# A tuned encoder layer: the transposed normalised input begins 192 bytes further on in its place

## The chip, the cores and the metric

The kernel runs on one core of one Trainium2 chip. A core has five engines that run side by side: TensorE (PE) multiplies matrices out of SBUF into PSUM, VectorE (DVE) and ScalarE (ACT) work element by element, GpSimd (POOL) does small vector work and issues some transfers, and SyncE (SP) issues most transfers. SBUF is the core's working memory: 128 partitions, each a row of bytes; a tile begins at the same byte in all of them. The metric is the device time of one execution in microseconds (us); of several runs the median counts.

## The reference

One layer of an encoder over 512 positions with 1024 channels, in float32. Its parts, shortened:

```python
u = rms_norm(h, g_mix)                       # (512, 1024)
z = u @ w_in                                 # one projection, columns split into:
q_a, k_a, v_a, q_b, k_b, v_b, f_b, gate_logits = split(z)
y_a = sliding_window_attention(q_a, k_a, v_a, sinks) @ w_br_swa
y_b = forgetting_attention(q_b, k_b, v_b, f_b + b_forget) @ w_br_fox
gates = sigmoid(gate_logits)                 # two per channel
h = h + (gates[0] * y_a + gates[1] * y_b) @ w_mix_out
u = rms_norm(h, g_mlp);  h = h + square(relu(u @ w_ff1)) @ w_ff2
h = h + sigmoid(rms_norm(h, g_ple) @ w_ple_gate) * (p @ w_ple_proj)
out = rms_norm(h, g_final)
```

Here it matters that the first `u` feeds every column of `w_in`: queries, keys, values, forget logits and gates.

## The kernel before

**Precision.** Every float32 operand of a large product is split into a rounded part `h` and a remainder `l`, and a product is three matmuls: high with high, high with low, low with high (`mm3`, lines 75 to 78). So `u` is kept transposed as two halves of one tile, `uh` and `ul`, each `[128 channels of a block, 8 blocks, 512 positions]`. This tile is called `u1` here; its name in the profile is `u`, as for the later `u2` and `u3`, which take the same place when it is free. Names such as `u25h` and `u25l` are something else: the split weights of unit 25. A unit is one weight block, and the units are prepared in a fixed order by `advance` and `emit_split` (ScalarE line 329, VectorE line 330).

**Stages in which `u1` is used.** The order of TensorE's instructions is written out by hand (`manual_schedule`).

1. *V stage*, until about 42 us. The input is normalised, transposed on TensorE (line 387) and written into `u1` by `hi_lo` (lines 72 and 73). `v_mm` (line 483) computes the values and forget logits: here blocks of `u1` are the weights that TensorE loads, and the tiles `wv_h` and `wv_l` stream through, 320 columns into `va` and 328 into `vb`, 192 matmuls in all.
2. *Prefetch*, `fill` with `mm3` into `pf`, lines 76 to 78, until 210 us. 21 chunks (keys, queries, and eight gate chunks), each of 8 blocks times 3 matmuls with 512 columns: a weight unit is loaded and a row block of `u1` streams through, 504 matmuls. The first 64 or so run in one piece; most of the others fill the gaps between the steps of sixteen attention heads (transposes line 827, scores line 769, values line 839), 9 to 18 at a time; the last two chunks run after the heads.
3. *Gates*, `win_mm`, line 918, from 232 to 271 us. The remaining gate columns are computed by a scheme with seven products (numbered `pn` 1 to 7) in place of eight, in blocks of 256 positions: 14 units of 24 matmuls with 256 columns. Products 1, 2 and 4 stream parts of `u1` itself (units 25, 26, 27, 30, 37, 38); products 5 and 6 stream the tile `u1_65` (units 28, 29, 31, 32), products 7 and 3 the tiles `u1_7` and `u1_3` (units 33 to 36), which `gate_ops` makes from `u1` on VectorE and ScalarE (lines 971 to 985, 72, 73).

After that the place is taken by `u_mix` (operands of the mix product, and one early weight block), by `u2` (the MLP's input) and at last by `u3`.

**Places.** Tiles get their bytes from pools that are stacked in order. As built, with the remainder of the first byte by 256:

| tile | first byte of the partition | remainder |
|---|---|---|
| `u1` (32 960 bytes, of which 32 768 hold data) | 17 088 | 192 |
| split weights `u0h`, `u0l`, ... (eight places, 4096 bytes apart) | 66 752 and on | 192 |
| `attn6` (attention output, streamed at lines 76 to 78 into `psy`) | 107 712 | 192 |
| `u1_65` | 182 144 | 128 |
| `u1_7`, `u1_3` | 140 992 and on | 192 |
| parts of `u_mix` | 17 088 + 192 and on | 128 |
| `wv_h`, `wv_l` | rows of 2592 bytes | eight different ones |

The place of `u1` is 48 words (`SHIFT`, 192 bytes) longer than its data. All row blocks of `u1` are 2048 bytes long, so each has the remainder of the first.

Of the kernel before, what the change touches and what calls it, by code (L numbers as in the profile page):

```python
# [15 lines left out]
S = 512  # L16
D = 1024
NT = S // P
KT = D // P
# [25 lines left out]
SHIFT = 48  # L45
# [7 lines left out]
def layer_kernel(ctx: ExitStack, tc: tile.TileContext, x, p, g_mix, w_in, b_forget, swa_sinks,  # L53
# [38 lines left out]
    def cols(w, c0, n, name):  # L92

        src = w[:, c0:c0 + n * P].rearrange("(k q) c -> q k c", q=P)
        r = add_raw([(slice(0, KT), src)], [P, KT, n * P], name)
        return [(r, (slice(None), slice(None), slice(j * P, (j + 1) * P)), [P, KT, P])
                for j in range(n)]
# [27 lines left out]
    for c2 in range(2):  # L125
        q = cols(w_in, C_QB + c2 * 256, 2, f"wqb{c2}")
        k = cols(w_in, C_KB + c2 * 256, 2, f"wkb{c2}")
# [271 lines left out]
    def new_uT(name):  # L399
        t = up.tile([P, 2 * KT * S + SHIFT], F32R, tag="u", bufs=1, name=name)  # L400
        if name == "u2":
            return t
        t = t[:, :2 * KT * S].rearrange("q (e k s) -> q e k s", e=2, k=KT)
        return t[:, 0], t[:, 1]


    psA = ctx.enter_context(tc.tile_pool(name="psA", bufs=2, space=PSUM))
    uh, ul = new_uT("u1")
    r_st = ctx.enter_context(ExitStack())
    glp = r_st.enter_context(tc.tile_pool(name="glp", bufs=1, side="right"))  # L410
# [82 lines left out]
    with tc.manual_schedule(engines={ET.Activation, ET.DVE, ET.SP}):  # L493
# [23 lines left out]
        for half in range(2):  # L517
            ps = psA.tile([P, S], F32, tag="sc", bufs=3, name=f"g_ps{half}")
            for j in range(4):
                k = half * 4 + j  # L520
# [625 lines left out]
    def new_u2():  # L1146

        u2 = new_uT("u2")
        n2 = 1024 + SHIFT
        for n, pn in enumerate((1, 4)):  # L1150
            first = [u2[:, 512 * n + 256 * e:512 * n + 256 * e + 256].rearrange("q (k s) -> q k s", k=1)
                     for e in range(2)]
            rest = [u2[:, n2 + 768 * e:n2 + 768 * e + 768].rearrange("q (k s) -> q k s", k=3)
                    for e in range(2)]
            u_op[pn] = [list(t) for t in zip(first, rest)]
            n2 += 1536
        for pn in (2, 6):
            u_op[pn] = [[u2[:, n2 + 1024 * e:n2 + 1024 * e + 1024].rearrange("q (k s) -> q k s", k=4)]
                        for e in range(2)]
            n2 += 2048  # L1160
# [217 lines left out]
    def t3(tb):  # L1378
        if tb == 0:
            u3["h"], u3["l"] = new_uT("u3")  # L1380
        to_uT(h_sb[:, tb, :], u3["h"], u3["l"], tb, psA, f"n3_{tb}", "sc")
# [109 lines left out]
    for n, st_ in enumerate(steps):  # L1491
        res = None
        if done is not None:
            if done[0] == "f1":
                res = win_out(done[:2], done[2], tmp)
                if res is not None:
                    src, dst, i, e = res
# [140 lines left out]
```

## Time and profile before

| | |
|---|---|
| median of 3 runs | 711.93 us (711.64 to 712.57) |
| profiled execution | 711.02 us, span from the first to the last instruction 709.3 us |
| mean granted clock of TensorE | 0.996 |
| busy: TensorE, its weight loads | 698.0 us (98%), 620.1 us (87%) |
| busy: VectorE, ScalarE, GpSimd | 551.2 us (78%), 457.2 us (64%), 88.7 us (13%) |
| matmuls | 4205 |

How its rows are read: a row of instructions gives line, engine, operation, `out<-in` by the program's tile names without buffer numbers, shapes, and the count; then busy time, mean duration in ns, and the idle time before them with what ended it. A timeline row begins with the start and the length in us. A matmul's duration holds its way through the array, and the next one begins before it ends; the distance between two starts is what it costs the engine. The chain of waits is the sequence of work that ended last, each piece reached from what released the next.

### The profile page before, as it was taken

The page shows a single profiled execution, that of the slowest core. Times are in us where ns is not written, and L with a number is a line of the kernel's source. Part 1 is how long each engine was busy: PE and PEld are TensorE (multiplying, and loading weights), DVE is VectorE, ACT ScalarE, POOL GpSimd, SP SyncE. Part 2 cuts the span into 40 slices and gives each one's busy share as a digit, 9 for nine tenths or more (in the row PEclk, how much of TensorE's full clock was granted, in tenths as well). Part 3 has the DMA queues.
Part 4 walks back from the last instruction along what each step waited for, and adds up shares of the span by engine and source line. Part 5 has one row for each costly group of instructions (what it writes and reads, how often), then busy time and mean ns, then how long its engine had stood idle before and what let it go on. Part 6 is the DMA issues. An engine that isn't in the chain of part 4 may idle for free.

```text
span 709.3 us, 11507 instructions
## 1 busy us (share of the span) xinstructions
PE 698.0 (98%) x4205; PEld 620.1 (87%) x4205; DVE 551.2 (78%) x942; ACT 457.2 (64%) x851; POOL 88.7 (13%) x128
## 2 busy tenths in 40 slices
PE   8999999999999999999999999999999999999996
PEld 7988888888888998888899889988998899988785
DVE  6557888876597666878999985899579966997565
ACT  6547888779962564447788646874487547875452
POOL 1011211100001200211300102010200020010101
PEclk9999999999999999999999999999999999999998
DMA  9256456670355798497885698739995699268003
GB/s 294 66 162 159 106 140 151 149 193 17 120 177 120 136 289 285 94 245 244 204 221 185 119 294 168 244 78 266 182 254 120 170 230 225 94 144 296 1 7 113
DMA packets 75288, 119.88 MB, mean 169 GB/s; under 512 B 6872, under 2 KB 44768, under 8 KB 75232
## 3 DMA queue, kind: packets, MB, share of 16 engines
q1 hardware_dynamic: 66016, 86.25, 38.7%
q0 software_dynamic: 8928, 32.51, 24.8%
q8 instruction: 33, 0.54, 0.3%
q10 hardware_dynamic: 288, 0.39, 0.2%
q14 instruction: 23, 0.19, 0.1%
HBM read 72.93 MB, written 4.19 MB: 109 GB/s over the span
## 4 chain that ended last, share of the span: by engine, by line
PE 89%; DVE 6%; issue 2%; DMA 2%; ACT 1%; POOL 0%; SPq 0%; POOLq 0%; DVEq 0%; ACTq 0%
PE pf L76 5%; PE pf L78 5%; PE pf L77 5%; PE (0, 's2')x L1304 3%; PE mxx L1304 3%; PE (2, 's2')x L1304 3%; PE (1, 's2')x L1304 3%; PE h_sc L769 3%; PE h_pv L839 2%; PE h_tr L827 2%; PE psy L76 2%; PE psy L78 2%; PE psy L77 2%; PE va L483 2%; PE vb L483 2%
## 5 line engine op out<-in xcount | busy, mean ns | idle before, releaser
L303 POOL DMA_DIRECT2D wq<-wq x35 | 30.4, 941 | 218.1 <-DVE u43l L330 30.5
L787 ACT ACTIVATE s<-s,h_nm 128x128 f32<-128x128 f32 (+1 forms) x64 | 32.6, 511 | 6.0 <-DVE h_nm L780 5.2
L73 DVE TENSOR_TENSOR h_ptl<-h_tr,h_pth 128x512 fp32r<-128x512 f32 (+2 forms) x40 | 22.9, 604 | 3.9 <-ACT h_pth L72 3.4
L72 ACT CAST h_pth<-h_tr 128x512 fp32r<-128x512 f32 (+2 forms) x40 | 19.5, 523 | 1.8 <-PE h_tr L827 1.5
L368 POOL TENSOR_SCALAR n_ms<-acc 128x1 f32<-128x1 f32 x15 | 6.9, 460 | 105.4 <-ACT junk L1136 45.8
L483 PE MATMUL va<-wv_h,u 128*128 128x320 f32 x64 | 20.0, 317 | 0.0
L303 POOL DMA_DIRECT2D wgw<-wgw x8 | 7.1, 968 | 101.6 <-DVE u25l L330 77.7
L827 PE MATMUL h_tr<-ident,s 128*128 128x128 f32 x136 | 19.6, 277 | 0.2
L483 PE MATMUL vb<-wv_h,u 128*128 128x328 f32 x64 | 19.6, 313 | 0.0
L839 PE MATMUL h_pv<-h_ptl,v 128*128 128x256 f32 (+1 forms) x64 | 16.9, 305 | 0.4 <-DVE h_ptl L73 0.3
L839 PE MATMUL h_pv<-h_pth,v 128*128 128x256 f32 (+1 forms) x64 | 17.3, 290 | 0.0
L1540 DVE TENSOR_TENSOR sgp<-sgp,pp 128x512 f32<-128x512 f32 (+1 forms) x9 | 5.7, 632 | 14.5 <-ACT sgp L1539 14.5
L827 PEld LDWEIGHTS h_tr<-ident,s 128*128 128x128 f32 x136 | 15.0, 141 | 2.0 <-DVE h_ao L849 0.5
L1136 ACT ACTIVATE junk<-h_sb 128x512 f32<-128x512 f32 x16 | 10.0, 631 | 9.7 <-DVE h_sb L1128 7.0
L807 ACT ACTIVATE s<-s,h_rec 128x128 f32<-128x128 f32 (+2 forms) x32 | 14.2, 482 | 2.3 <-DVE h_rec L801 2.3
L849 DVE TENSOR_TENSOR h_ao<-h_pv,h_ao 64x512 f32<-64x512 f32 x16 | 10.9, 682 | 6.1 <-ACT h_ao L848 5.8
L801 DVE RECIPROCAL h_rec<-h_den 128x4 f32<-128x4 f32 x16 | 3.0, 185 | 14.5 <-ACT s L787 14.3
L775 DVE CUSTOM_DVE_ANT_0 s<-h_sc,causal 128x128 f32<-128x128 f32 (+3 forms) x32 | 13.8, 484 | 0.3 <-PE h_sc L769 0.3
L1539 ACT ACTIVATE sgp<-psgt,rs 128x512 f32<-128x512 f32 x7 | 4.8, 685 | 14.2 <-PE psgt L78 14.2
L839 PEld LDWEIGHTS h_pv<-h_ptl,v 128*128 128x128 f32 x64 | 12.1, 188 | 1.7 <-DVE h_ptl L73 0.8
L73 DVE TENSOR_TENSOR u<-n_tr,u 128x512 fp32r<-128x512 f32 x16 | 10.5, 685 | 3.9 <-ACT u L72 3.9
L775 DVE CUSTOM_DVE_ANT_0 s<-h_sc,bswa 128x256 f32<-128x256 f32 (+1 forms) x32 | 10.7, 384 | 3.1 <-PE h_sc L769 3.1
(1645 smaller groups left out, 2779.9 us busy)
## 6 DMA issues: line engine op xcount, KB each, us to landing
wq<-in_w_ff_dram SPq DMA_DIRECT2D x43, 512.0 KB, 5.9
wq<-wq POOLq DMA_DIRECT2D x35, 512.0 KB, 5.6
wq_c<-in_w_ff_dram SPq DMA_DIRECT2D x9, 512.0 KB, 6.2
wg<-in_w_in_dram SPq DMA_DIRECT2D x4, 1024.0 KB, 5.6
wgw<-in_w_in_dram SPq DMA_DIRECT2D x8, 512.0 KB, 4.9
wgw<-wgw POOLq DMA_DIRECT2D x8, 512.0 KB, 5.8
wq<-in_w_mix_out_dram SPq DMA_DIRECT2D x8, 512.0 KB, 5.2
wpg<-in_w_ple_gate_dram SPq DMA_DIRECT2D x4, 1024.0 KB, 7.7
```

The lines of the kernel that those rows point to most:

```text
L73: nc.vector.tensor_tensor(lo, src, hi.bitcast(F32), ALU.subtract)
L76: nc.tensor.matmul(ps, lh, rh, start=start, stop=False)
L77: nc.tensor.matmul(ps, lh, rl, start=False, stop=False)
L78: nc.tensor.matmul(ps, ll, rh, start=False, stop=stop)
L303: nc.gpsimd.dma_start(q, other, accum_op=ALU.add)
L483: nc.tensor.matmul(ps, u[:, kk_, ts_], w[:, kk_, c0:c1], start=kk_ == 0 and n == 0, stop=kk_ == KT - 1 and n == 2)
L769: nc.tensor.matmul(ps[:, off:off + n], qs[i][z][:, qb * P:(qb + 1) * P], kk[i][z][:, k0:k0 + n], start=z == 0, stop=z == 1)
L775: nc.vector.tensor_tensor_reduce(out=s[:, o:o + n], in0=ps[:, off:off + n], in1=c["bias"](qb), scale=1.0, scalar=NEG, op0=ALU.add, op1=ALU ...
L787: nc.scalar.activation(sl, sl, AF.Exp, bias=nm[:, qb:qb + 1], accum_out=den[:, qb:qb + 1])
L827: nc.tensor.transpose(tr[:, n, :], c["s"][:, o, :], ident)
L839: nc.tensor.matmul(pv[:, q0:q0 + nq, :], V2[kb][:, c["v"], :], t[:, o:o + nq, :], start=n == 0, stop=n == 2 * NT - 1, skip_group_check=True)
L1304: nc.tensor.matmul(bank[bkey, bk, i], o, w, start=tg != "" and n == 0, stop=n == 5, skip_group_check=True)
```

## The change

`new_uT` makes the tile of the transposed input and cuts it into `uh` and `ul`. For `u1` the cut now begins at word 48 of the place in place of word 0; `u3` begins at word 0 as before.

```diff
     def new_uT(name):
         t = up.tile([P, 2 * KT * S + SHIFT], F32R, tag="u", bufs=1, name=name)
         if name == "u2":
             return t
-        t = t[:, :2 * KT * S].rearrange("q (e k s) -> q e k s", e=2, k=KT)
+        n = SHIFT if name == "u1" else 0
+        t = t[:, n:n + 2 * KT * S].rearrange("q (e k s) -> q e k s", e=2, k=KT)
         return t[:, 0], t[:, 1]
```

`u1` then begins at byte 17 280, with remainder 128. Every other tile stays where it was. The program has the same instructions in the same order with the same waits; in 840 matmuls, 16 VectorE and 8 ScalarE instructions the address of the operand in `u1` is 48 words higher.

## The prediction

> **What bounds the kernel now.** I read the busy times first, then the waits of TensorE, then the chain of waits, and last the timeline of single matmuls.
>
> ```profile
> PE 698.0 (98%) x4205; PEld 620.1 (87%) x4205; DVE 551.2 (78%) x942; ACT 457.2 (64%) x851; POOL 88.7 (13%) x128
> ...
> PE 89%; DVE 6%; issue 2%; DMA 2%; ACT 1%; POOL 0%; SPq 0%; POOLq 0%; DVEq 0%; ACTq 0%
> ```
>
> TensorE (PE) is busy 98% of the span and holds 89% of the chain that ended last. The tile `u1` is in use until 271 us, so the next rows are TensorE's stretches there (us, busy, matmuls, clock, DMA share, GB/s) and its only wait between 40 and 272 us.
>
> ```profile
> 40.00:56.00 16.00, 16.00 (x77) 1.00 0.55 136
> 56.00:199.00 143.00, 142.42 (x795) 1.00 0.48 125
> 199.00:231.00 32.00, 32.00 (x143) 1.00 0.60 165
> 231.00:271.00 40.00, 40.00 (x337) 1.00 0.87 234
> PE h_pv L839 <- DVE h_ptl L73: 0.3, 1, 0.3
> ```
>
> TensorE idles 0.6 us of 231, at the full granted clock. So in this part one matmul follows the other as fast as TensorE takes them, and a nanosecond more or less on each goes to the end time one for one. The question is therefore only what the new address does to the distance from the start of one matmul to the start of the next. The printed durations (389 ns for 512 columns) overlap each other; I use the distance between starts.
>
> **The change part by part.** The two programs have the same instructions in the same order. 864 of them reach `u1` 48 words further on: 840 matmuls, 16 VectorE and 8 ScalarE instructions. No wait, transfer or tile is added or moved. I write an operand's place as its start byte modulo 256, moving operand first, weights second. `u1` goes from 192 to 128; the weight units `u0h`, `u0l` and so on stay at 192.
>
> *First term: the gate matmuls with 256 columns (line 918).* Of 336, 144 stream `u1` itself (units 25, 26, 27, 30, 37, 38), so they go from 192/192 to 128/192. The trace already has both pairs in this stage: units 28, 29, 31 and 32 stream `u1_65`, which lies at 128. Here is the chain of waits, 24 matmuls a row.
>
> ```profile
> 234.76 2.88 PE ('g', 1, 2)x L918 x24
> 237.64 2.88 PE ('g', 0, 2)y L918 x24
> 240.52 2.74 PE ('g', 0, 2)z L918 x24
> 243.26 2.72 PE ('g', 1, 2)z L918 x24
> 245.98 2.86 PE ('g', 1, 2)y L918 x24
> 265.80 2.88 PE ('g', 0, 2)x L918 x24
> ```
>
> Rows 3 and 4 are units 28 and 29: 2.72/24 = 113.3 ns, against 2.88/24 = 120 ns for `u1` (119.2 in unit 30). Units 33 to 36, whose moving tiles lie at 192, take 2.88 too. Over the six `u1` units the starts give 119.8 ns on average, so the gain is 144 x (119.8 - 113.5) = 0.9 us. Could something else become late? TensorE never waits in this stage, and the engines that prepare its weights have room; below are TensorE, its weight loads, VectorE, ScalarE and GpSimd.
>
> ```profile
> 231.00:271.00 40.00, 40.00 (x337) 39.84 (x337) 26.47 (x31) 23.85 (x39) 5.17 (x6) 1.00 0.87 234
> ```
>
> VectorE is busy 26.5 of 40 us and ScalarE 23.9. They must finish each 24-matmul unit 0.15 us sooner, which they do where units 28, 29, 31 and 32 run. If a transfer were late instead (the DMA engines are at 87%), the most that is lost is this 0.9 us.
>
> *Second term: the prefetch matmuls `pf` with 512 columns (lines 76 to 78).* There are 21 chunks of 24, 504 in all, and all of them stream `u1`: 192/192 now, 128/192 then. First what they take now, from the timeline: first start and first start behind the stretch.
>
> ```profile
> 41.78 0.40 PE L76 MATMUL pf<-u,u0h 128*128 128x512 f32 x1
> ...
> 56.09 0.39 PE L76 MATMUL pf<-u,u2h 128*128 128x512 f32 x1
> ...
> 134.08 0.48 PE L76 MATMUL pf<-u,u11h 128*128 128x512 f32 x1
> 134.40 0.40 PE L77 MATMUL pf<-u,u11h 128*128 128x512 f32 x1
> 134.63 0.40 PE L78 MATMUL pf<-u,u11l 128*128 128x512 f32 x1
> 134.87 0.40 PE L76 MATMUL pf<-u,u11h 128*128 128x512 f32 x1
> ...
> 199.09 0.39 PE L76 MATMUL pf<-u,u19h 128*128 128x512 f32 x1
> ...
> 209.97 0.39 PE L76 MATMUL psy<-attn,u21h 128*128 128x512 f32 x1
> ```
>
> In the first stretch 63 matmuls take 14.31 us, 227.2 ns each; in the last 48 take 10.88 us, 226.7 each. In the fills between the attention heads it is less even: behind a transpose the first one takes about 314 (the row at 134.08), and the next ones 224 to 236 until they settle at 227. Added up over all starts: 484 ordinary ones at a mean of 228.8 ns (63 at 227.2, 373 at 229.3, 48 at 226.7), and 20 long ones that follow a transpose and that I leave as they are.
>
> What 128/192 takes at 512 columns is shown in one place only. In the mix stage `u_mix` holds one weight block at 128, streamed against weights at 192, and its rows even agree with the changed `u1` in the byte modulo 2048 (896).
>
> ```profile
> 301.37 2.96 PE L1304 MATMUL mxz<-u_mix,mo 128*128 128x512 f32 x12
> 304.17 0.40 PE L1304 MATMUL mxy<-u47h,u_mix 128*128 128x512 f32 x1
> L1304 PE MATMUL mxz<-u_mix,mo x12: 394/394/397, 301.4 to 303.9; 128*128 128x512 f32 x12
> L1304 PE MATMUL mxx<-u45h,u_mix x8: 388/390/394, 298.6 to 301.1; 128*128 128x512 f32 x8
> L1304 PE MATMUL mxy<-u47h,u_mix x8: 396/397/398, 304.2 to 306.7; 128*128 128x512 f32 x8
> L78 PE MATMUL pf<-u,u1l x8: 389/389/389, 47.7 to 52.5; 128*128 128x512 f32 x8
> ```
>
> The twelve take 304.17 - 301.37 = 2.80 us, 233.3 each, all alike. So the pair that is the quick one at 256 columns is the slow one at 512. I take 233.3: the bytes are the same and so is the number of columns. The cost is 484 x (233.3 - 228.8) = 2.2 us. The bounds come from the nearest rows. Below: no steady stretch of 512 columns is under 226.7, which gives 484 x (226.7 - 228.8) = -1.0 us. Above: 236, the longest that keeps coming back in the fills, gives +3.5 us. Between them lies the mirrored pair 192/128: the row of `u45h` is a mixture of 226, 229 and 232 (229 on average) and the row of `u47h` a steady 233. So two rhythms are possible for one pair, and which one comes depends on what ran ahead. At 229.7 the term would be +0.4 us.
>
> *Third term: the V stage (line 483), where `u1` is the weights.* 192 matmuls load their weights from `u1`; the moving tiles `wv_h` and `wv_l` have rows of 2592 bytes, so the eight row blocks start at eight different places, 32 bytes apart modulo 256.
>
> ```profile
> L483 PE MATMUL va<-wv_h,u x64: 303/311/416, 8.9 to 41.5; 128*128 128x320 f32 x64
> L483 PE MATMUL vb<-wv_h,u x64: 308/312/320, 9.2 to 41.6; 128*128 128x328 f32 x64
> ```
>
> All eight pairs stand in these rows, and the medians of the starts lie within 146 to 150 ns for `va` and 149 to 155 for `vb`. If the distance between the two places counts, moving `u1` by 64 modulo 256 only exchanges the eight distances among the eight blocks; if the moving place counts, it does not change. Both give zero. Bounds: 192 x 5 ns = 1.0 us either way.
>
> *Fourth: the 24 VectorE and ScalarE instructions.* They write `u1` in the V stage and read it for the gate operands.
>
> ```profile
> L73 DVE TENSOR_TENSOR h_ptl<-h_tr,h_pth 128x512 fp32r<-128x512 f32 x24 | 15.8, 683 | 2.1 <-ACT h_pth L72 1.9
> L73 DVE TENSOR_TENSOR u<-n_tr,u 128x512 fp32r<-128x512 f32 x16 | 10.5, 685 | 3.9 <-ACT u L72 3.9
> ```
>
> `h_ptl` lies at 32 and `u` at 192, with the same instruction and the same 683 to 685 ns: I cost it at zero. It also runs beside TensorE work. Were it 5 ns more on each of the 24, that would be 0.1 us even without cover.
>
> The Trainium skill speaks against any effect at all. In "SBUF — State Buffer" (Specifications) it gives 16-byte lines in SBUF, and 192 bytes are twelve whole lines; in "TensorE: Matmul & The Clock Gate" (Part 2: What happens when you issue a matmul, step 1) it says that TensorE reads the weights and the moving operand through two independent ports, so loading the next weights takes nothing from a running matmul. By these the sum would be zero. The trace does not agree: the rows at 240.52 and 245.98 have equal shapes and equal weights' places, and differ by 0.12 us in 24 matmuls.
>
> **The sum.** -0.9 (gates) + 2.2 (`pf`) + 0 + 0 = +1.3 us. The profiled execution took 711.02 us with a span of 709.3; it would become 712.3 with a span of 710.6. It lies 0.9 us under the median of the three runs, 711.93, so the median becomes **713.2 us**. A measurement of this kernel tells about 0.2% (1.4 us) from no change, so the forecast lies just inside "no change", on the slow side.
>
> **The rivals.**
>
> *A. `pf` finds the better rhythm.* Between 229.7 (+0.4 us) and 226.7 (-1.0 us) for `pf`, with the gates' -0.9: -0.5 to -1.9 us, 711.4 to 710.0. For it: the row of `u45h`, where a pair with different places ran at 229, and the fills, which settle at their best rhythm after some ten matmuls. Against it: all twelve of `u_mix` were slow from the first, although they followed `u45`'s mixture.
>
> *B. Slower: the weights' place costs too.* In the V stage every matmul would take one step (6.7 ns) more once its weights lie at 128, as `u47h` with weights at 128 takes 233 against 227: 192 x 6.7 = 1.3 us on top, +2.6 us, 714.5. It decides as soon as it is above 0.1 us, since the rest stands at +1.3. For it: no row of `u_mix` as weights has a median below 390, where plain rows have 389. Against it: the V stage has eight pairs already and none stands out by more than 5 ns.
>
> *C. The place does not matter for 512 columns, nor by itself for 256; what differs is the tile.* Then nothing happens: 711.9. This is the reading to which the two rules of the Trainium skill above lead. For it: only `u_mix` shows the slow pair. Against it: units 33 to 36, other tiles at 192, run at 120 as `u1` does.
>
> *D. `pf` loses a step.* At 256 columns 128/192 takes 6.7 ns less; were it so at 512 (220 ns), `pf` would give 484 x 8.8 = -4.3 us and with the gates -5.2: 706.7. Against it: no stretch of 512 columns anywhere settles under 226.7.
>
> **How the numbers follow.** Forecast 0.52, A 0.26, B 0.11, C 0.07, D 0.04. The forecast's own range, 712.4 to 714.0, lies across the 0.2% bound at 713.35; I give 0.29 of it to no change and 0.23 to slower. A gives 0.14 to no change and 0.12 to faster, B 0.11 to slower, C 0.07 to no change, D 0.04 to faster. Together: faster 0.16, the same 0.50, slower 0.34. The range runs from the good end of A, 710.0, to the forecast's upper edge with B, 714.7; about 0.2 is left outside with D, the edges and the spread of the runs.
>
> **What would show it.** The gate units of `u1` at 2.72 to 2.74 us per 24 in the chain of waits (right) or still 2.88. The `pf` stretch of units 19 and 20: 11.2 us from its first start to that of `psy` (right), 10.9 (A or C) or 10.6 (D). The V stage's rows unchanged in their medians (right) or 5 to 7 ns up (B). The forecast is wrong if `pf` keeps its 389 ns, or if TensorE shows waits between 40 and 272 us that it does not have now.

## The result, and the profile after

The changed kernel takes **714.17 us** (median of 7 runs, 713.34 to 715.51), the kernel before 711.93 beside it (7 runs, 710.51 to 712.77): ratio 1.0034, 95% interval 1.0024 to 1.0044. So it is slower, by 1.7 to 3.1 us by the interval, which is more than the 0.2% that a measurement tells from no change. Predicted were 713.2 us, in a range of 710.0 to 714.7. The profiled execution took 714.12 us with a span of 712.4 (before: 711.02 and 709.3). Of the runs further below, two single ones that took far longer (869.77 us with `u1` at place 0, 2485.57 us with `u1` and the weights moved) are in no ratio.

The busy times from the profile's page, and then TensorE's only wait between 40 and 272 us (who waited, for whom, us in total, times, longest). The insertion of one line shifts the code below it: line 918 is now 919, 839 is 840, 483 is 484; lines 76 to 78 stay.

```profile
PE 701.1 (98%) x4205; PEld 620.8 (87%) x4205; DVE 552.0 (77%) x942; ACT 457.5 (64%) x851; POOL 89.2 (13%) x128
```

```profile
PE h_pv L840 <- DVE h_ptl L73: 0.3, 1, 0.3
```

TensorE is busy 3.1 us longer and the same single 0.3 us wait stands where it stood: nothing has begun to wait in the part that uses `u1`. The time went into the matmuls. First the `pf` stretch of units 19 and 20, from its first start to the first start behind it (timeline: start, printed duration).

```profile
200.67 0.39 PE L76 MATMUL pf<-u,u19h 128*128 128x512 f32 x1
200.90 0.39 PE L77 MATMUL pf<-u,u19h 128*128 128x512 f32 x1
201.14 0.39 PE L78 MATMUL pf<-u,u19l 128*128 128x512 f32 x1
...
211.87 0.39 PE L76 MATMUL psy<-attn,u21h 128*128 128x512 f32 x1
```

48 matmuls take 11.20 us, 233.3 ns each; before they took 10.88, 226.7 each. The gate stage, from the chain of waits (start, us, what; 24 matmuls are one unit; the rows are the units 26, 27, 28, 29 and 37):

```profile
236.64 2.83 PE ('g', 1, 2)x L919 x24
239.47 2.83 PE ('g', 0, 2)y L919 x24
242.29 2.83 PE ('g', 0, 2)z L919 x24
245.12 2.83 PE ('g', 1, 2)z L919 x24
...
267.94 2.74 PE ('g', 0, 2)x L919 x24
```

Units 26 and 27 (rows 1 and 2) went from 2.88 to 2.83 us, and only units 37 (last row) and 38 reach the forecast 2.72 to 2.74. Units 28 and 29 (rows 3 and 4), whose operand `u1_65` was not touched, went the other way, from 2.74 and 2.72 to 2.83. The V stage, where `u1` is the weights, has the same durations within 3 ns in the medians:

```profile
L484 PE MATMUL va<-wv_h,u x64: 303/309/417, 9.0 to 41.8; 128*128 128x320 f32 x64
L484 PE MATMUL vb<-wv_h,u x64: 308/312/320, 9.2 to 41.9; 128*128 128x328 f32 x64
```

The same matmuls matched one to one between the two traces give the delay as it grows: +0.28 us at 34 us, +0.68 at 71, +1.40 at 179, +1.93 at 220 and at 249, +1.83 at 274, +1.82 still at 507; then +2.05 at 529, +2.77 at 618 and +3.09 at 702. At 34 us neither a `pf` nor a gate matmul has run (the V stage has; its 192 starts sum to 30.45 us against 30.34), and behind 271 us no instruction touches `u1`. So between 34 and 274 us the delay grows by 1.83 - 0.28 = 1.55 us, and another 1.3 us arise behind 507 us. The waits of TensorE behind 505 us, first before, then after:

```profile
PE psgt L77 <- DVE u173l L321: 0.3, 1, 0.3
```

```profile
PE psgt L77 <- DVE u173l L321: 0.7, 2, 0.4
PE ('f1', 6)x L919 <- ACT u_('f1', 6)_6525 L930: 0.4, 1, 0.4
```

Some 0.8 us of the late part are these two waits. Whether the change causes them is one of the questions below.

### The profile page after: what moved, and what is told of

It is laid out like the page before. It is cut to its first block, busy times and chain, and to the rows that moved or that the text cites. A ratio compares the mean times of both kernels' runs of the same rounds, so it can differ in the third digit from the quotient of the medians.

```text
span 712.4 us, 11507 instructions
## 1 busy us (share of the span) xinstructions
PE 701.1 (98%) x4205; PEld 620.8 (87%) x4205; DVE 552.0 (77%) x942; ACT 457.5 (64%) x851; POOL 89.2 (13%) x128
## 4 chain that ended last, share of the span: by engine, by line
PE 76%; DVE 10%; issue 5%; DMA 4%; ACT 3%; POOL 1%; SPq 0%; POOLq 0%; ACTq 0%; DVEq 0%
PE pf L76 5%; PE pf L77 5%; PE pf L78 5%; PE (0, 's2')x L1305 3%; PE mxx L1305 3%; PE (1, 's2')x L1305 3%; PE psy L76 2%; PE psy L78 2%; PE psy L77 2%; DMA wq<-wq 2%; PE h_pv L840 2%; PE h_sc L770 2%; PE h_tr L828 2%; PE vb L484 2%; PE va L484 2%
```

## The experiments

Three questions: what property of an address sets the rhythm of the matmuls, that is the even distance between their starts; why the gate units did not take the rhythm that the same pair of places had shown before; and whether the delay behind 507 us belongs to the change. As in the prediction, a place is the start byte modulo 256, moving operand first, weights second; the *distance* is the first less the second. Theory **D** says that the distance decides; its rival **M** that the moving operand's own place does.

### The same kernel again: what chance does

The kernel before, unchanged.

> The kernel before once more, for the spread of its profile. Theory 'the part after 271 us is chance': the stages after 271 us differ from the first profile by up to 1 us, as they do between the two kernels (1.3 us later in the changed one), and the pf and gate stages do not differ at all. Rival 'the later part is an effect of the change': they agree with the first profile within 0.3 us.

Median 711.62, ratio 1.0002 (0.9989 to 1.0014). Matched with the first profile of before, its start times run +0.27 us apart at 34 us, +0.18 at 274, -0.12 at 507 and +0.43 at 702. So differences of some 0.3 us at the beginning, as much between 274 and 507 us, and 0.55 us behind 507 come without any change. From 274 to 702 us they nearly cancel (+0.25 us), so this run alone does not decide between the two expectations; the repeated run of the changed kernel, at the end, does more. `pf` and the gates repeat to a nanosecond in the mean (226.7 in units 19 and 20, 119.9 in units 25 to 27).

### u1 at two other places

```diff
-        n = SHIFT if name == "u1" else 0
+        n = 16 if name == "u1" else 0
```

(and 32 in the second run; 16 words are 64 bytes.)

> u1 begins 64 bytes further on than before (remainder 0 in place of 192; the weights stay at 192). Theory D, the distance between the moving place and the weights' place sets the rhythm: the distance is now +64, that of the mirrored pair 192/128 in the mix stage, so the pf matmuls settle at 229 to 233 ns, units 19 and 20 take 11.0 to 11.2 us, and the time is 712.3 to 714.2 us. Theory M, the moving operand's own place counts, multiples of 128 bytes being slow at 512 columns and quick at 256: pf at 233.3 as in the changed kernel, u1's gate units at 113 to 118 ns, 714.2 us.

> u1 begins 128 bytes further on than before (remainder 64; weights at 192). Theory M: an odd multiple of 64 bytes, so as before: pf settles at 226.7 ns, u1's gate units at 120 ns, 711.9 us. Theory D: the distance is 128, which no stage shows; anything between 226.7 and 233.3 ns for pf, that is 711 to 714.2 us, but there is no reason for the gate units to stay at just 120 ns.

At 0/192 (distance +64) the `pf` stretch in the timeline, and unit 26 in the chain of waits:

```profile
199.88 0.39 PE L76 MATMUL pf<-u,u19h 128*128 128x512 f32 x1
...
210.87 0.40 PE L76 MATMUL psy<-attn,u21h 128*128 128x512 f32 x1
```

```profile
235.67 2.83 PE ('g', 1, 2)x L919 x24
```

At 64/192 (distance 128) the same two views, with unit 28 on `u1_65` as a second row of the chain:

```profile
200.41 0.40 PE L76 MATMUL pf<-u,u19h 128*128 128x512 f32 x1
...
211.56 0.39 PE L76 MATMUL psy<-attn,u21h 128*128 128x512 f32 x1
```

```profile
236.36 2.88 PE ('g', 1, 2)x L919 x24
...
242.12 2.74 PE ('g', 0, 2)z L919 x24
```

10.99 us (228.9 ns) and 11.15 us (232.2 ns). M asked for 233.3 at place 0 and 226.7 at place 64, and neither came. The 228.9 is the average of the mirrored pair in the mix stage (units 45, 50 and 54). The gate units, though, came as M had asked: 117.8 ns at place 0 and 119.9 at place 64, where D saw no reason for just 120. The totals: 712.09, ratio 1.0007 (0.9998 to 1.0017), which is a little under D's range, and 713.35, ratio 1.0024 (1.0014 to 1.0033). D stands by the `pf` stretch alone, and these two runs would also fit a table of places of the moving operand.

### The other operand moved

A pad ahead of the weights' pool moves the weight units by 192 bytes; a later pad of that size is dropped. With it come the tile that `attn6` and later `at_ff` use, and a few later pools; `u1`, `u_mix` and `u2`, whose place lies ahead of the pad, stay. Once on the changed kernel (`u1` 128, weights 128) and once on the kernel before (192, 128).

```diff
     sm = ctx.enter_context(tc.tile_pool(name="sm", bufs=2))
+    sm.tile([P, SHIFT], F32, name="line_w", bufs=1)
...
-    at2.tile([P, SHIFT], F32, name="line_b")
```

> The changed kernel, with the weight units (and the tile with remainder 192 that attn6 lies in, and the attention output) also moved, so that u1 and the weights stand at 128/128: another absolute place than 192/192, but the same distance of zero. Theory D (the distance between moving operand and weights sets the rhythm): pf goes back to 226.7 ns, units 19 and 20 take 10.88 us, the gate units of u1 take 120 ns (2.88 us per 24), the total is that of the kernel before within 0.2%. Theory M (the place of the moving operand alone): pf stays at 233.3, 11.20 us, total as the changed kernel.

> The kernel before, with only the weight units (and attn6, attention output) moved, u1 untouched: 192/128. No instruction reaches u1 at another address than before. Theory D: the distance is now +64, as with u1 at 0 and the weights at 192, so pf takes 228.9 ns (units 19 and 20: 10.99 us) and the gate units of u1 117.8 ns. Theory M: u1 stands where it stood, so 226.7 (10.88 us) and 120 ns (2.88 us per 24).

The changed kernel with moved weights (its lines stand one further down): `pf` in the timeline, then the units 26, 28 and 29 in the chain of waits.

```profile
199.45 0.39 PE L77 MATMUL pf<-u,u19h 128*128 128x512 f32 x1
...
210.33 0.39 PE L77 MATMUL psy<-attn,u21h 128*128 128x512 f32 x1
```

```profile
235.13 2.88 PE ('g', 1, 2)x L919 x24
...
240.89 2.88 PE ('g', 0, 2)z L919 x24
243.77 2.88 PE ('g', 1, 2)z L919 x24
```

10.88 us, 226.7 ns: with `u1` at the changed place, the old rhythm is back in full. And units 28 and 29, which read `u1_65` at 128 in every run here, now stand at distance zero and take 2.88 instead of 2.72 to 2.74. The kernel before with moved weights, the same two views (unit 26):

```profile
199.30 0.39 PE L77 MATMUL pf<-u,u19h 128*128 128x512 f32 x1
...
210.29 0.40 PE L77 MATMUL psy<-attn,u21h 128*128 128x512 f32 x1
```

```profile
235.09 2.83 PE ('g', 1, 2)x L918 x24
```

10.99 us, 228.9 ns, and 2.83: no access to `u1` changed, yet the numbers are those of the run with `u1` at 0. M is refuted twice over.

The totals miss the expectation, though: 716.44 us for the first of the two (ratio 1.0072, 1.0054 to 1.0091), and 715.78 for the single run of the second. The pad put other operands at new distances as well, which I had not counted. Between two starts the 672 `f1` matmuls on `u2` went from 113.7 ns at distance -64 to 119.9 at zero; the chain of waits, before and with the pad:

```profile
424.35 2.77 PE ('f1', 2)x L918 x24
427.12 2.76 PE ('f1', 3)x L918 x24
```

```profile
425.40 2.87 PE ('f1', 2)x L919 x24
428.27 2.87 PE ('f1', 3)x L919 x24
```

Over all 1344 `f1` matmuls the starts sum to 157.4 us against 153.4 (+4.0); `psg` at the end gives +0.9 (its 512-column matmuls now at -64 take 233), the gates +0.6, and the mix stage, whose pairs all came to zero, -0.4. Together +5.1, which is the measured 0.72% of 711.6. This is the theory at work in stages that it was not made from, though `f1` alone scatters by up to 1 us between runs without a pad. The 576 `f1` matmuls on `at_ff`, which moved with the weights from 128/192 to 64/128 and so kept the distance -64, kept their 113.6 ns.

### One period further, and half a line

First the pad as 256 bytes on the kernel before, with the two later pads dropped:

```diff
+    sm.tile([P, 64], F32, name="line_w", bufs=1)
...
-    sm3.tile([P, 16], F32, name="line_c")
...
-    at2.tile([P, SHIFT], F32, name="line_b")
```

> The kernel before with the weight units and all that is allocated behind them moved by 256 bytes instead of 192, u1 untouched: 192/192 again, one period further. Theory D with a period of 256 bytes: nothing changes anywhere, pf 226.7 ns (10.88 us for units 19 and 20), gate units of u1 120 ns, the mix stage 38.7 us, the f1 matmuls 153.4 to 154.3 us (they took 157.4 when the weights moved by 192), total within 0.2% of before. If the period is longer (512 or more), pf moves to another rhythm, 228.9 to 233.3 ns; if the moved tiles cost by themselves, the f1 matmuls stay near 157.

`pf` 10.88 us, units 25 to 27 119.9 ns, `f1` 153.3 us: 256 bytes are a whole period, and moved tiles cost nothing by themselves. Dropping the pad `line_c` had a side effect that the expectation did not foresee: the operands of units 33 to 36 came to 128 and the weights of the `s2` matmuls too, and both followed their distances. Units 33 and 34 in its chain of waits:

```profile
254.32 2.72 PE ('g', 0, 2)x L917 x24
257.04 2.72 PE ('g', 0, 2)z L917 x24
```

They took 2.88; in all four units the gain is 0.6 us, while the `s2` matmuls, now at +64, went from a mean of 227.7 to 229.1 ns, +0.9 us. The single total is 711.10 against 711.18.

The same side effect shows more in the mix stage. The mirrored pair 192/128 of units 47 and 48 is the same as before, but the twelve matmuls ahead of it (`mxz<-u_mix,mo`) came to distance zero and ran at 227.7 ns on average instead of 233.3.

```profile
L1303 PE MATMUL mxy<-u47h,u_mix x8: 388/392/397, 303.5 to 306.1; 128*128 128x512 f32 x8
```

This row had 396/397/398 before. The 24 starts of units 47 and 48 were 233.3 ns apart on average before and are 229.6 now, a mixture of 226, 229 and 232. So at 512 columns, too, one pair has two rhythms, and what ran ahead chooses between them.

Then `u1` only 32 bytes further on (n = 8 in the first diff), 224/192:

> u1 begins 32 bytes further on instead of 192: it stands at 224, the weights at 192, distance +32. Two theories of how fine the distance counts. D64 (in steps of 64 bytes): +32 lies in the same step as 0, pf takes 226.7 ns (units 19 and 20: 10.88 us) and the gate units of u1 120 ns. D32 (finer): something between the 226.7 at 0 and the 228.9 at +64, or another rhythm altogether, for instance 227.5 to 228.5 ns (10.92 to 10.97 us).

The `pf` stretch in the timeline, and unit 26 in the chain of waits:

```profile
200.40 0.40 PE L76 MATMUL pf<-u,u19h 128*128 128x512 f32 x1
...
211.60 0.40 PE L76 MATMUL psy<-attn,u21h 128*128 128x512 f32 x1
```

```profile
236.36 2.80 PE ('g', 1, 2)x L919 x24
```

D64 is refuted, and D32's figures of 227.5 to 228.5 ns were missed as well: 11.20 us, 233.3 ns, the slowest value, at the smallest distance; units 25 to 27 take 116.7 ns, a value seen nowhere else. So 32 bytes count, and the cost does not grow with the distance. Only one run stands behind the value at +32, so that it belongs to the distance rather than to the place 224 is not shown.

| u1/weights | distance | `pf`, units 19, 20 (ns) | units 25–27 (ns) | 28, 29 | 37, 38 |
|---|---|---|---|---|---|
| 192/192 before | 0 | 226.7 | 119.9 | 113.7 | 120.0 |
| 192/192, one period on | 0 | 226.7 | 119.9 | 113.7 | 119.6 |
| 128/128 | 0 | 226.6 | 119.9 | 120.0 | 120.0 |
| 224/192 | +32 | 233.3 | 116.7 | 117.8 | 117.9 |
| 0/192 | +64 | 228.9 | 117.8 | 117.7 | 117.9 |
| 192/128 | +64 | 228.9 | 117.8 | 120.0 | 117.9 |
| 64/192 | 128 | 232.2 | 119.9 | 113.7 | 118.8 |
| 128/192 changed | -64 | 233.3 | 117.8 | 117.8 | 113.7 |

(Means of the distances between starts. `u1_65`, the operand of 28, 29, 31 and 32, lies at 128 throughout.)

### What ran ahead

In the changed kernel units 25 and 28 have the places that ran at 113.3 ns before, and run at 117.8. The first idea was that any interruption ahead of them frees them; four transposes, whose result nobody reads, are put ahead of the first gate unit.

```diff
+        if t == ("g", 0, 2, 1):
+            gap = psA.tile([P, 4, P], F32, tag="tr", bufs=3, name="gap")
+            for j in range(4):
+                nc.tensor.transpose(gap[:, j, :], ident, ident)
```

> The changed kernel with four transposes of the identity matrix, whose result nobody reads, between the branch products and the first gate unit. Theory H, the rhythm at 256 columns depends on what ran ahead (in the changed kernel the first eight gate units run at 117.8 ns although four of them, at the same places, ran at 113.4 before): the transposes break the rhythm, the first eight units run at 113.4 ns, 24 x 8 x 4.4 ns = 0.85 us less, against 0.44 us for four transposes, 713.8 us. Rival, 117.8 ns is what u1's new place costs in this stage: the units keep 117.8 ns and the time is 0.4 us longer, 714.6 us.

The chain of waits, with the last transpose and units 25 and 26:

```profile
233.91 0.11 PE gap L1089
234.02 2.83 PE ('g', 0, 2)x L919 x24
236.84 2.83 PE ('g', 1, 2)x L919 x24
```

It does not: 2.83 from the first unit on. The total, 713.21 (ratio 1.0024, 1.0015 to 1.0033), lies under both expected values, 713.8 and 714.6, and decides nothing here. The rows of before suggest another reading: there units 28 and 29 followed a steady stretch of 120 ns, and after the change unit 37, which follows 120 ns, is the one that reaches 113.7. So 16 matmuls of 256 columns at distance zero, again read by nobody, are put in that place.

```diff
+            if t == ("g", 0, 2, 1):
+                lead = psA.tile([P, S], F32, tag="tr", bufs=3, name="lead")
+                for j in range(16):
+                    nc.tensor.matmul(lead[:, 0:256], order[i][2][0][:, j % 4, j // 4 % 2, :],
+                                     attn_t(0)[0][:, 0:256], start=True, stop=True)
```

> The changed kernel with 16 more matmuls of 256 columns ahead of the first gate unit, moving operand (the first attention output) and weights both at 192, result unread: work added, about 16 x 120 = 1.9 us. Theory H2 (at 128/192 two rhythms, 113.3 and 117.8 ns, exist and the one is kept that the matmuls ahead led into; from a steady 120 ns stretch it is 113.3, from the 512-column stretch 117.8): units 25 to 32 take 113.3 to 113.8 ns each instead of 117.8, 2.72 us per 24, so 0.8 us are won back of the 1.9. Rival: what ran ahead does not matter, units 25 to 32 keep 117.8 ns (2.83 us per 24) and the added 1.9 us stand in full.

The chain of waits, with the added matmuls and the units 25 to 29:

```profile
233.95 1.56 PE lead L1106 x13
235.51 2.74 PE ('g', 0, 2)x L919 x24
238.25 2.72 PE ('g', 1, 2)x L919 x24
240.97 2.72 PE ('g', 0, 2)y L919 x24
243.69 2.72 PE ('g', 0, 2)z L919 x24
246.41 2.72 PE ('g', 1, 2)z L919 x24
```

2.72 us in all the units from 26 to 32, with no other edit: the gate units sum to 27.24 us (without 33 to 36) against 28.07 in the changed kernel, -0.83 us. The pair 128/192 at 256 columns has two rhythms, 113.3 and 117.8 ns, and keeps for eight units the one that it was led into. A steady 120 ns is not the only lead-in to the quick one: with `u1` at 224 units 28 and 29 ran at 117.8 ns behind units at 116.7, and units 31 and 32 at 113.6 behind one at 116.8. What exactly chooses is open. The 1.9 us of added work cost more than that; its single time is 715.78 us.

### The mix stage at distance zero

If D holds, the kernel before can be made quicker: its `u_mix` blocks lie at 128 beside weights at 192, and go back to 192.

```diff
-        n = (1, 2, 5, 6, 3, 7).index(pn) * 1024 + SHIFT
+        n = (1, 2, 5, 6, 3, 7).index(pn) * 1024
...
-                                     for n in (6144 + SHIFT, 7168 + SHIFT)]
+                                     for n in (6144, 7168)]
```

> The kernel before, with the u_mix blocks that lie at 128 (and the mirrored weights) moved back by 192 bytes to 192, so that every matmul of the mix stage stands at distance zero. Theory D: its matmuls go from a mean of 229.5 ns to 226.7 to 227.5, the stage from 38.73 us to some 38.3, total 0.3 to 0.5 us below the kernel before (ratio 0.9994), less than the measurement tells from none. If the place of one operand alone counted, the mix stage would keep 229.5 ns.

Two of the groups of the mix line that the prediction quoted (printed durations, least, median, longest):

```profile
L1304 PE MATMUL mxz<-u_mix,mo x12: 388/389/390, 301.5 to 304.0; 128*128 128x512 f32 x12
L1304 PE MATMUL mxy<-u47h,u_mix x8: 389/389/390, 304.3 to 306.8; 128*128 128x512 f32 x8
```

The rows that had 394 and 397 ns have 389, the starts sum to 38.35 us for the 168 matmuls instead of 38.73. In the total that cannot be seen: 711.94 us against 711.57, ratio 1.0001 (0.9991 to 1.0012). It beats neither kernel by what can be measured.

### The changed kernel once more

> The changed kernel once more, unchanged. Up to 271 us its matmuls cost about 1.8 us more than before (pf +2.0, gates -0.1, the rest near zero), but the profiled executions differ by 3.1 us and the medians by 2.4. Theory 'chance': the part behind 271 us is scatter of late waits, so the ratio comes out near 1.0025 (+1.8 us) and this profile starts its late stages at another offset. Theory 'real': the delay also makes something late behind 271 us, so the ratio is 1.0034 or more again and the growth between 515 and 601 us comes back.

Median 713.14 us against 711.52, ratio 1.0032 (1.0017 to 1.0047). The ratio is near the 1.0034 that the theory 'real' asked for, but one long run of the ten, 718.04 us, is in it; the medians are 1.6 us apart, and the means without that run 1.7. The profiled execution has a span of 711.1, 1.8 above before. Matched with before, its starts are -0.12 us apart at 34 us, +1.43 at 274, +1.52 from 467 to 594 and +1.79 at 702; `f1` sums to 153.3 us, as before (the first profile of after: 154.3), and TensorE's waits behind 505 us are now

```profile
PE psgt L77 <- DVE u173l L321: 0.6, 2, 0.3
```

The wait in front of `f1` is gone, and with it the growth between 515 and 618 us. That part was chance: `f1` also sums to 153.8 us in the repeated kernel before and to 154.1 in the mix experiment, where `u1` was not moved. From 34 to 274 us this trace gives 1.43 + 0.12 = 1.55 us, the same as the first, where the kernel before, repeated, gives -0.09: this is the effect of the change.

## Why the prediction was right, and where it was not

**What bounds the kernel** was read rightly: TensorE back to back from 40 to 272 us, so each nanosecond on a matmul reached the end. The unchanged wait row shows it, and the delay stayed at +1.82 us from 274 to 507 us.

**The second term** (`pf`) was right in value and size. Forecast were 233.3 ns; measured are 233.4 in the first stretch, 233.0 in the fills, 233.3 in units 19 and 20: 63 x 6.2 + 373 x 3.7 + 48 x 6.6 = 2.1 us against 2.2 forecast. The choice of the byte-equal row `u_mix` over the mirrored pair was the right one, and the experiments say why: the mirrored pair is another distance (+64) and tells nothing of this one. That the mirrored pair itself has two rhythms, as the prediction read from `u45h` and `u47h`, holds, as the run moved by one period shows. Rival A is out by the measured 233 ns in all three stretches. What the term did not contain: the matmuls right behind a fill (`h_pv`) start 10 ns closer together than before (median 224 against 234), and those that follow them a little closer as well, so that the attention heads' own matmuls sum to 50.12 us against 50.49, and 50.09 in the repeated run. That gives 0.4 us back. It is no scatter: the six traces with `pf` at 232 to 233 ns have 50.05 to 50.15 us, the seven others 50.43 to 50.54; why was not looked into.

**The first term** (gates, -0.9 us) failed; measured is -0.1. The step that failed is the one that took the 113.3 ns of units 28, 29, 31 and 32 as the property of their places. They are one of two rhythms of this pair, and in the changed kernel this pair comes straight behind 512-column matmuls, where before it came behind units at 120 ns. Units 25, 26, 27, 30, 37 and 38 gained 0.5 us of the 0.9, and the four untouched units on `u1_65` lost 0.4, which the prediction had not considered. The prediction did say, of 512 columns, that the rhythm may depend on what ran ahead, but did not apply it here. With a lead-in of 120 ns the six units take 8.18 + 2.72 + 5.46 = 16.36 us against 17.25 before: exactly the 0.9 us.

**The third term** (V stage, zero) was right: its 192 starts sum to 30.45 and 30.26 us against 30.34, and rival B, 1.3 us on top, is out. **Rival C** (the place does not matter) is refuted by every run that moved one operand alone. The Trainium skill's two rules that spoke for it, 16-byte lines in "SBUF — State Buffer" (Specifications) and two independent ports in "TensorE: Matmul & The Clock Gate" (Part 2: What happens when you issue a matmul, step 1), give no change for 192 bytes, as the prediction took them together; here the `pf` starts went from 226.7 to 233.3 ns, so for this shape the trace does not agree. **Rival D** (220 ns) never appeared.

**The sum.** +2.1 (`pf`) - 0.4 (behind the fills) - 0.1 (gates) = +1.6 us, and the two traces give 1.55; predicted were +1.3. The gates came out 0.8 us dearer than forecast and the heads' own matmuls 0.4 us cheaper, so that the sum is off by only 0.3 us is in part luck. The effect lies at 0.22%, just above the bound that the prediction gave for no change, which it held the likeliest outcome (0.50, against 0.34 for slower). The medians of the first measurement are 2.2 us apart, of the second 1.6. The rest is most likely scatter of the late stages; but the interval of the first measurement begins at 1.7 us, so that a few tenths come from elsewhere is not excluded.

## What to carry to other kernels

A kernel that is bound by matmuls back to back can win or lose some tenths of a per cent with the start address of an operand alone, with not an instruction changed; read it from the distances between starts in the timeline, since printed durations overlap (389 ns printed where the starts are 226.7 ns apart). Compare both operands' start bytes modulo 256, and take the price from a row with the same pair, the same columns and the same work ahead of it. Where allocations are padded to bring one pair to a good distance, list every other pair that the pad moves: here one pad put `u1` right and cost 5 us elsewhere.

## What the runs showed of the hardware

All of this is for FP32R matmuls with 128 rows and 128 weight columns, each with its own weight load, at a granted clock of 1.00 (the stages from 40 to 600 us).

- The distance between starts depends on the start bytes of moving operand and weights relative to each other, modulo 256. At 512 columns: 226.7 ns at distance 0 (192/192 and 128/128, and one period on), 228.9 at +64 (0/192 and 192/128; behind matmuls at 233 the latter took 233.3 as well), 232.2 at 128 and 233.3 at -64 (one pair of places each), and 233.3 in the one run at +32. The order is not that of the distance; why is open.
- At 256 columns the good distance is another: 120 ns at 0, 117.8 at +64, and at -64 113.3 or 117.8 (at 128 119.9 or 118.8, at +32 116.7 or 117.9, each in one run). So `f1` (256 columns) and `pf` (512) cannot share a weights' place that is best for both with operands at one place.
- A rhythm outlives what began it: at -64 it was kept through eight units, 192 matmuls, whichever it was. Four transposes ahead did not change it, 16 matmuls at 120 ns did. At 512 columns the pair 192/128 kept 233.3 ns through two units, 24 matmuls, behind others at 233, and took 229.6 where those ahead ran at 227.7. The mechanism behind it was not looked into.
